# Mixer projections in blocks of 1024 columns, two of eight k-tile pairs with seven products, PE and ACT in a hand-written order, two sums moved to accumulating DMA

## The chip, the cores and the metric

One core of a Trainium2 chip runs the whole program. The metric is the device time of one execution in microseconds (us), the median of three runs. The core's engines work side by side and wait for each other through semaphores: TensorE (PE, matmuls and transposes), VectorE (DVE), ScalarE (ACT), GpSimd (POOL), and SyncE (SP), which here only issues the loads of weights. Operands lie in SBUF, results of PE in 8 banks of PSUM, each 128 partitions x 512 float32. All DMA queues share 16 DMA engines.

## The reference

One residual block on 256 tokens, model width 2048, float32:

```python
u = rms_norm(h, g_mix)
q, k, v, q_idx, k_idx, w_idx, z, xbc, dt_raw = split(u @ w_in)
y_attn = dsa_attention(rope(q), rope(k), v, rope(q_idx), rope(k_idx), w_idx)
# Mamba-2: conv and silu on xbc -> xs (4096 wide), B, C; 8 groups of 8 heads of 64, state 128
decay = exp(where(causal, acum[:, None] - acum[None, :], -inf))
y = (C B^T * decay) @ (xs * dt) + d_skip * xs
y = y * silu(z);  y_ssm = y * rsqrt(mean(y*y over the group) + eps) * g_norm
gates = sigmoid(u @ w_gate)
h = h + (gates[0] * (y_attn @ w_attn_branch) + gates[1] * (y_ssm @ w_ssm_branch)) @ w_out
h = h + (silu(gate) * up) @ w_ffn_out      # gate, up = split(rms_norm(h) @ w_ffn_in)
out = rms_norm(h, g_final)
```

The scan over chunks of 64 is computed in the kernel as one causal 256 x 256 product per head: three 128 x 128 tiles of decay a head, 128 x 384.

## The kernel before

**A projection.** 256 tokens are two row blocks (t) of 128; 2048 rows of a weight are 16 k-tiles of 128. The activation tile is the stationary operand, 512 columns of a weight are the moving one, and each product is made of three matmuls, hi x hi, hi x lo and lo x hi, so that float32 precision is kept. `gemm` makes 512 columns for both row blocks, in chunks of 4 k-tiles (1 MB): SP loads `raw`, ACT copies it to `hi` (L196, two 128x1024 copies a chunk), DVE subtracts `lo` (L197), PE does L165, L166 and L167 for each k-tile and row block (24 matmuls a chunk of 128x512). Four `mm` banks hold two gemms, so that one is read while the next is made; two banks (`tr`) take transposes, two (`sd`) small products. Four pairs of `hi`/`lo` tiles are in turn. In this text a *block* is 1024 columns of a projection, a *group* one of the 8 SSM groups, and `ssm_out` the product of a group's output with its 512 rows of w_ssm_branch (`w_sb`): 96 matmuls.

**The order of the work.** The program is written as a straight sequence, and Tile's scheduler orders each engine's instructions, with the weight loads and splits at high priority. The sequence: the small columns of w_in (`w_a`), then B and C (2048 columns of `w_m`), the index columns (`w_i`, two gemms of 384), eight groups (the x gemm of the group, `ssm_out` of the group before, the z gemm), k and v, four attention blocks (a q gemm of 512, a gate gemm of 512, the attention of 4 heads), `w_g` gates, `w_ab`, `w_o`, and the feed-forward block (FFN).

**The FFN's sevens.** In the FFN (`w_f`, L696 to L900) most chunks are made with seven products in place of eight for each 2 x 2 set of tiles (Strassen-Winograd): DVE forms differences of weight tiles (`ta` L749, `tb` L750, each then split like a weight, L730 and L731) and later adds the banks of the products together (L876). Its matmuls are L808 and its transposes L846. The change does not touch this code.

**A group's decay, `ssm_x`.** The running sums `acum` of a group's 8 heads lie in DRAM; POOL loads them to all partitions (`abc`), DVE forms 24 differences of 128x128, ACT takes the exponential, DVE multiplies by the masked scores `cbm`:

```python
nc.gpsimd.dma_start(abc..., acum_d[g * HPG : (g + 1) * HPG, :]...partition_broadcast(P))      # L481
nc.vector.tensor_scalar(E[:, hh, lo : lo + P], av[:, ao : ao + P], dcols[:, i, h : h + 1], 0.0, op, ALU.min)   # L504, 24 a group
nc.scalar.activation(E, E, AF.Exp)                                                             # L507, 128x1536, 2 a group
nc.vector.tensor_tensor(E, E, cbm.unsqueeze(1).broadcast_to([P, 4, 384]), ALU.mult)            # L508
```

**A group's output.** `y*y` is summed over 512 columns (L547 and a small matmul), POOL makes 1/sqrt of it (`rsg`, L133 to L144), and `ssm_out` scales its banks by it while it adds them to `acc`, which stays in SBUF over all groups:

```python
nc.scalar.activation(a, ps[t], AF.Copy, scale=r[:, t : t + 1])                  # L561, group 0
nc.vector.scalar_tensor_tensor(a, ps[t], r[:, t : t + 1], a, ALU.mult, ALU.add) # L563, groups 1 to 7
```

Of the kernel before, what the change touches and what calls it, by code (L numbers as in the profile page):

```python
# [41 lines left out]

C_GM = 0
# [21 lines left out]
def hybrid_block(ctx, tc, xt, x, consts, cols, heads, gfin, w_a, w_i, w_m, w_g, w_ab, w_sb, w_o, w_f1, w_f2, out):  # L65
# [12 lines left out]
    dp = ctx.enter_context(tc.tile_pool(name="dp", bufs=1, space=bass.MemoryType.DRAM))  # L78
    pctx = ctx.enter_context(ExitStack())
# [22 lines left out]
    def sd_t(shape, name="sd"):  # L102
        return sdp.tile(shape, F32, tag="sd", name=nm(name))
# [16 lines left out]
    tri = kc[:, K_TRI : K_TRI + P]  # L120
# [26 lines left out]
    xtra = []  # L147
    turn = [0]

    def hl_tiles():  # L150
        turn[0] += 1
        if xtra and turn[0] % 5 == 0:
            return xtra[0].tile([P, 1024], F32R, tag="hi", name=nm("hi")), xtra[0].tile([P, 1024], F32R, tag="lo", name=nm("lo"))
        return whi.tile([P, 1024], F32R, tag="hi", name=nm("hi")), wlo.tile([P, 1024], F32R, tag="lo", name=nm("lo"))

    def gemm(w, first, N, nk, lhs, before=None, late=0):


        ps = [mm.tile([P, 512], F32, tag="mm", name=nm("mm")) for _ in range(T)]
# [76 lines left out]
    u_hi = [big_t([P, 8, S], F32R, name="uh") for _ in range(2)]  # L236
    u_lo = [big_t([P, 8, S], F32R, name="ul") for _ in range(2)]

    def u_chunk(c, part=0):

        if c == 0:
            ks = (0, 2) if part == 0 else (2, 4)
        else:
            ks = (4 * c, 4 * c + 4)
        with tc.high_priority(PRE):
            load_xt(*ks)
            if c == 0 and part == 0:
# [28 lines left out]
    ps = gemm(w_a, 0, 400, KT, lhs_u, u_chunk)  # L276
# [17 lines left out]
    with tc.high_priority(PRE):  # L294
        sqp = sd_t([P, T])
        for t in range(T):
            for i in range(2):
                nc.tensor.matmul(sqp[:, t : t + 1], part[:, i, t * P : (t + 1) * P], onec, start=(i == 0), stop=(i == 1))
        ssq = sm.tile([P, T], F32, tag="ssq", name="ssq_x")
        nc.vector.tensor_copy(ssq, sqp)  # L300
        nc.vector.tensor_copy(rstd, rstd_of(ssq, D, "rs0"))
# [30 lines left out]
    wk0 = mid_t([P, 1024], name="wk0")  # L332
    wk1 = mid_t([P, 1024], name="wk1")
    kdup = wk0[:, 0:256].rearrange("p (t n) -> p t n", t=T)
    dtok = wk0[:, 256:384].rearrange("p (t n) -> p t n", t=T)
    dl, e1, rest = wk0[:SH, 384:640], wk0[:SH, 640:896], wk0[:SH, 896:1024]
    r1, r2, ones, ea = wk1[:SH, 0:256], wk1[:SH, 256:512], wk1[:SH, 512:640], wk1[:SH, 640:641]
    qi_a = mid_t([P, T, 256], name="qia")
    for t in range(T):
        nc.scalar.activation(dtok[:, t, :], ps[t][:, 336:400], AF.Copy, scale=rs(t))  # L340
        nc.scalar.activation(widx[:, t, :], ps[t][:, 320:336], AF.Copy, scale=rs(t))
        rope_apply(kdup[:, t, 0:64], ps[t][:, 256:320], t, 1, 32)
        nc.vector.tensor_copy(kdup[:, t, 64:128], kdup[:, t, 0:64])
# [3 lines left out]
    tp = tr_t([P, S])
    for t in range(T):
        nc.tensor.transpose(tp[:SH, t * P : (t + 1) * P], dtok[:, t, :], ident)
    nc.scalar.activation(dl, tp[:SH, :], AF.Identity, bias=headp[:, 0:1])  # L350
    nc.scalar.activation(e1, dl, AF.Abs)
    nc.scalar.activation(e1, e1, AF.Exp, scale=-1.0)
    nc.scalar.activation(ea, headp[:, 1:2], AF.Exp)
    nc.vector.tensor_scalar_add(r1, e1, 2.0)
    nc.vector.reciprocal(r1, r1)
    nc.vector.tensor_tensor(r1, r1, e1, ALU.mult)
    nc.vector.tensor_tensor(r2, r1, r1, ALU.mult)
# [10 lines left out]
    nc.vector.tensor_scalar(rest, dl[:, 0:P], -1.0, dl[:, P - 1 : P], ALU.mult, ALU.add)
    acum_d = dp.tile([SH, S], F32, name="acum_d")
    nc.gpsimd.dma_start(acum_d, dl)  # L370
    tp = tr_t([P, 5, SH])
    for i, src in enumerate((r1[:, 0:P], r1[:, P:S], dl[:, 0:P], dl[:, P:S], rest)):
        nc.tensor.transpose(tp[:, i, :], src, ident[:SH, :SH])
    dcols = cp.tile([P, 5, SH], F32, name="dcols")
    nc.vector.tensor_copy(dcols, tp)


    kbd = mid_t([P, 2, S], name="kbd")
    nc.gpsimd.memset(kbd, 0.0)
    tp = tr_t([P, S])  # L380
    for t in range(T):
        nc.tensor.transpose(tp[:, t * P : (t + 1) * P], kdup[:, t, :], ident)
    nc.vector.tensor_copy(kbd[0:64, 0, :], tp[0:64, :])
    nc.vector.tensor_copy(kbd[64:128, 1, :], tp[64:128, :])
    kbd_h = mid_t([P, 2, S], F32R, name="kbdh")
    kbd_l = mid_t([P, 2, S], F32R, name="kbdl")
    split(kbd_h, kbd_l, kbd)
# [28 lines left out]

    index_pairs(qi_a, 2, 12)


    def conv_block(ps, cb, dst):  # L420

        xk = ev_t([P, T, 512], "xk")
        for t in range(T):
            nc.scalar.activation(xk[:, t, :], ps[t], AF.Copy, scale=rs(t))
        for h in range(2):
            tp = tr_t([P, 2, S])
            for c in range(2):
                for t in range(T):
                    o = (2 * h + c) * P
                    nc.tensor.transpose(tp[:, c, t * P : (t + 1) * P], xk[:, t, o : o + P], ident)  # L430
            for c in range(2):
                ch = cb * 4 + 2 * h + c
                a = dst[:, 2 * h + c, :]
                nc.scalar.activation(a, tp[:, c, :], AF.Identity, scale=ccol(C_CW, 3 * 48 + ch), bias=ccol(C_CB, ch))
# [131 lines left out]
    for g in range(GROUPS):  # L566
# [3 lines left out]
        if pend is not None:  # L570
            ssm_out(*pend)
# [495 lines left out]
```

## Time and profile before

| | before |
|---|---|
| time, median of 3 runs | 1971.53 us (1970.67 to 1971.98) |
| span of the profiled execution | 1967.9 us |
| PE busy | 1954.5 us (99%) |
| DVE busy | 1499.9 us (76%) |
| ACT busy | 1066.8 us (54%) |
| POOL busy | 36.2 us (2%) |
| moved by DMA | 375.71 MB, mean 191 GB/s |

The span is 3.6 us under the median. In the span the stages lie so: `w_a`, B, C and index to about 185 us, eight groups to 748 (each takes 72.2 us), k and v to 820, attention to 1021, gates to 1108, `w_ab` to 1172, `w_o` to 1256, FFN to the end. In a group of rows, "x424 | 517.7, 1223 | 310.4" means 424 instructions, 517.7 us busy in all, 1223 ns for one by itself, and 310.4 us of idle time of that engine just ahead of them. One by itself can be longer than its part of the busy time, since an instruction begins before the one ahead has wholly ended. In a table by windows each row gives the busy time of PE, of the weight loads (PEld), DVE, ACT and POOL, then the granted clock of PE, the busy share of the DMA engines and what they moved in GB/s.

### The profile page before, as it was taken

To read this page: it belongs to the slowest core of one execution; us is meant where nothing else is said; L and a number is where in the kernel's file an instruction comes from. 1 tells how busy PE (TensorE), PEld (TensorE's weight loads), DVE (VectorE), ACT (ScalarE), POOL (GpSimd) and SP (SyncE) were. 2 spreads that over 40 slices of the span, in tenths; PEclk is the share of its full clock that TensorE was granted. 3 is DMA by queue.
4 is the path that set the end of the run, shared out by engine and by line. 5 is a ranking of instruction groups with operands and counts; after the bars stand their busy time and mean duration, and the time that the engine had idled before them with its cause. 6 is when DMAs were issued, how large, how long until landed. Compare 5 with 4: busy or idle time off the path is not lost. (4 is left out here: it accounts for less than half of the span.)

```text
span 1967.9 us, 23619 instructions
## 1 busy us (share of the span) xinstructions
PE 1954.5 (99%) x9095; PEld 1619.2 (82%) x9095; DVE 1499.9 (76%) x2050; ACT 1066.8 (54%) x1291; POOL 36.2 (2%) x87
## 2 busy tenths in 40 slices
PE   9999999999999999999999999999999999999998
PEld 7898888888888888888888888788888888888886
DVE  7898867778778766666654556788989999899964
ACT  6575564654654544555554445565555665555553
POOL 0000000000000000000000000000000000000000
PEclk9999999999999999999999999999999999999999
DMA  7645555555554545544555555455545555555553
GB/s 276 233 151 177 189 195 187 190 195 171 193 203 160 193 171 192 182 163 168 185 185 195 184 193 206 154 198 212 193 178 208 213 194 213 192 195 213 212 193 128
DMA packets 54432, 375.71 MB, mean 191 GB/s; under 512 B 6304, under 2 KB 6816, under 8 KB 10672
## 3 DMA queue, kind: packets, MB, share of 16 engines
q1 hardware_dynamic: 51120, 360.86, 51.8%
q0 software_dynamic: 1968, 11.60, 1.7%
q10 hardware_dynamic: 1232, 1.75, 0.2%
q8 instruction: 71, 1.16, 0.2%
q14 instruction: 41, 0.34, 0.1%
HBM read 372.02 MB, written 2.16 MB: 190 GB/s over the span
## 5 line engine op out<-in xcount | busy, mean ns | idle before, releaser
L197 DVE TENSOR_TENSOR lo<-raw,hi 128x1024 fp32r<-128x1024 f32 (+3 forms) x449 | 540.5, 1207 | 314.6 <-ACT hi L196 313.1
L196 ACT ACTIVATE hi<-raw 128x1024 fp32r<-128x1024 f32 (+3 forms) x449 | 468.8, 1047 | 529.9 <-PE mm L167 463.4
L166 PE MATMUL mm<-lo,uh 128*128 128x512 f32 (+2 forms) x1184 | 461.0, 389 | 0.0
L167 PE MATMUL mm<-hi,ul 128*128 128x512 f32 (+2 forms) x1184 | 458.2, 388 | 0.2 <-DVE ul L218 0.2
L165 PE MATMUL mm<-hi,uh 128*128 128x512 f32 (+2 forms) x1184 | 453.2, 389 | 1.0 <-ACT hi L196 1.0
L730 ACT ACTIVATE hi<-raw 128x1024 fp32r<-128x1024 f32 x240 | 232.8, 978 | 138.7 <-PE p L808 103.0
L808 PE MATMUL p<-hi,opa 128*128 128x512 f32 x924 | 306.4, 390 | 0.0
L731 DVE TENSOR_TENSOR lo<-raw,hi 128x1024 fp32r<-128x1024 f32 x240 | 265.0, 1119 | 19.9 <-ACT hi L730 19.1
L165 PEld LDWEIGHTS mm<-hi,uh 128*128 128x128 f32 x1184 | 222.5, 188 | 44.5 <-ACT hi L196 1.9
L167 PEld LDWEIGHTS mm<-hi,ul 128*128 128x128 f32 x1184 | 222.8, 188 | 42.5 <-DVE ul L218 0.5
L166 PEld LDWEIGHTS mm<-lo,uh 128*128 128x128 f32 x1184 | 222.9, 188 | 41.0 <-DVE lo L197 0.3
L808 PEld LDWEIGHTS p<-hi,opa 128*128 128x128 f32 x924 | 173.4, 188 | 35.6
L808 PE MATMUL p<-lo,opa 128*128 128x512 f32 x462 | 180.9, 392 | 0.7 <-DVE lo L731 0.7
L808 PE MATMUL p<-hi,act 128*128 128x512 f32 x416 | 132.5, 390 | 0.0
L808 PE MATMUL p<-hi,opb 128*128 128x512 f32 x352 | 127.2, 391 | 1.0 <-ACT opf L695 0.8
L808 PEld LDWEIGHTS p<-lo,opa 128*128 128x128 f32 x462 | 86.7, 188 | 19.7 <-DVE lo L731 1.9
L166 PE MATMUL mm<-lo,yh 128*128 128x512 f32 x256 | 100.4, 392 | 0.0
L167 PE MATMUL mm<-hi,yl 128*128 128x512 f32 x256 | 100.4, 392 | 0.0
L165 PE MATMUL mm<-hi,yh 128*128 128x512 f32 x256 | 100.1, 395 | 0.0
L808 PEld LDWEIGHTS p<-hi,act 128*128 128x128 f32 x416 | 78.1, 188 | 16.4 <-ACT hi L730 0.3
L730 ACT ACTIVATE hi<-tb 128x1024 fp32r<-128x1024 f32 x45 | 47.7, 1059 | 76.7 <-PE p L808 45.7
L808 PE MATMUL p<-lo,act 128*128 128x512 f32 x208 | 80.6, 391 | 0.0
(283 smaller groups left out, 2533.2 us busy)
## 6 DMA issues: line engine op xcount, KB each, us to landing
raw<-in_w_f_dram SPq DMA_DIRECT2D x132, 1024.0 KB, 4.8
raw<-in_w_m_dram SPq DMA_DIRECT2D x104, 1024.0 KB, 4.8
raw<-in_w_sb_dram SPq DMA_DIRECT2D x32, 1024.0 KB, 4.8
raw<-in_w_g_dram SPq DMA_DIRECT2D x32, 1024.0 KB, 4.8
raw<-in_w_ab_dram SPq DMA_DIRECT2D x16, 1024.0 KB, 4.8
raw<-in_w_o_dram SPq DMA_DIRECT2D x16, 1024.0 KB, 4.8
abc<-acum_d POOLq DMA_DIRECT2D x8, 1024.0 KB, 5.2
raw<-in_w_i_dram SPq DMA_DIRECT2D x8, 768.0 KB, 4.3
```

The costliest lines, as they stand in the source:

```text
L165: nc.tensor.matmul(o, lh, rh, start=(kt == 0), stop=False)
L166: nc.tensor.matmul(o, lh, rl, start=False, stop=False)
L167: nc.tensor.matmul(o, ll, rh, start=False, stop=(kt == nk - 1))
L196: hi_ops.append(nc.scalar.activation(hi[:, o], src[:, o], AF.Copy))
L197: nc.vector.tensor_tensor(lo[:, o], src[:, o], hi[:, o].bitcast(F32), ALU.subtract)
L730: nc.scalar.activation(hi, src, AF.Copy)
L731: nc.vector.tensor_tensor(lo, src, hi.bitcast(F32), ALU.subtract)
L808: nc.tensor.matmul(ps[i], x, y, start=start and j == 0, stop=left[i] == 0)
```

## The change

All projections of u (`w_m`, `w_i`, `w_g`) are made in blocks of 1024 (`w_i`: 768) columns; q and the gate columns of an attention block share one block, as do x and z of a group. A block is made as a 2 x 2 set of results: two row blocks by two column halves, in all four `mm` banks. Its 16 k-tiles are four quads of 4, each two chunks of 1 MB; ORDER sets the order of the eight chunks, and MIX marks quads 0 and 1, whose first chunk (one pair of k-tiles) is made with 7 products of three matmuls instead of 8 (`sevens`). Four of the seven products go to banks of their own (1, 5, 6, 7), which are the four `trp` banks; `sdp` is gone, and transposes and small products share `trp`. DVE adds the banks together at the end of the block (`add`). The first two blocks (B and C) are plain; 15 blocks of 1024 and the one of 768 have sevens.

`ssm_out` is made as two plain blocks of 1024 columns. ACT copies its scaled banks to `sums`, and POOL adds these by an accumulating DMA to `acc_d` in DRAM, which is read back after the last group. The decay starts from a mask that a DMA loads into `E`; a second, accumulating DMA adds the rows of `acum`, and ACT takes the exponential with the per-partition part as a bias, 16 instructions a group. The masked score product is one ACT copy. The sum of squares of x comes from loads of x and ACT's accumulator, not from transposed squares and small matmuls; that of y from two adds.

PE and ACT run in the order in which the program is written (`manual_schedule`); the steps of a group are generators that are resumed after counted matmuls (`tick`). DVE, POOL and SP are ordered by the scheduler as before. FFN, `w_ab` and `w_o` keep their code, without the extra `hi`/`lo` pair that came in every fifth time.

```diff
+MIX = (1, 1, 0, 0)
+ORDER = ((2, 0), (2, 1), (0, 0), (1, 0), (0, 1), (1, 1), (3, 0), (3, 1))
+NHL = 5
...
-    whi = ctx.enter_context(tc.tile_pool(name="whi", bufs=4))
-    wlo = ctx.enter_context(tc.tile_pool(name="wlo", bufs=4))
+    whi = ctx.enter_context(tc.tile_pool(name="whi", bufs=NHL))
+    wlo = ctx.enter_context(tc.tile_pool(name="wlo", bufs=NHL))
-    ev = ctx.enter_context(tc.tile_pool(name="ev", bufs=2))
+    ev = ctx.enter_context(tc.tile_pool(name="ev", bufs=4))
...
-    trp = pctx.enter_context(tc.tile_pool(name="trp", bufs=2, space=bass.MemoryType.PSUM))
-    sdp = pctx.enter_context(tc.tile_pool(name="sdp", bufs=2, space=bass.MemoryType.PSUM))
+    trp = pctx.enter_context(tc.tile_pool(name="trp", bufs=4, space=bass.MemoryType.PSUM))
...
+    manual.enter_context(tc.manual_schedule(engines={mybir.EngineType.PE, mybir.EngineType.Activation}))
...
+            if seven:
+                yield from ask()
+                flush()
+                ta, tb = (mid_t([P, 1024], name="ts")[:, : 2 * N] for _ in range(2))
+                nc.vector.tensor_tensor(ta, tile_of(2, 2), tile_of(1, 2), ALU.subtract)
+                part(tile_of(0, 2), 0, 1)
...
+                part(ta, 4, 5)
+                nc.vector.tensor_tensor(tb[:, :N], tile_of(3), ta[:, :N], ALU.subtract)
+                nc.vector.tensor_tensor(tb[:, N:], tile_of(0), tb[:, :N], ALU.subtract)
...
+                part(tb, 6, 7)
...
+                part(tile_of(3), 3)
...
+        for x, part in ((a[0], 0), (a[0], 1), (a[1], 0)):
+            for c, b in uses:
+                left[c] -= 1
+                nc.tensor.matmul(ps[c], x, b[part], start=c in begun, stop=left[c] == 0)
...
+            for m, (c, l, r) in enumerate(((1, 0, 1), ((0, 0), 2, 0), (7, 1, 5), (5, 8, 4), (6, 9, 6), ((1, 0), 3, 7), ((0, 1), 12, 3))):
+                products(ps, left, get, op_u(q, l), [(c, operand(n, r))])
...
+                    if c == 1:
...
+                        nc.scalar.activation(x[1], ps[1], AF.Copy)
+                    elif c == 6:
+                        add(2, 6, 1)
+                        add(3, 7, 2)
+                        add(4, 5, 3)
+                        add(2, 5, 2)
...
+        xin = [big_t([P, D], name="xin") for _ in range(T)]
+        for t in range(T):
+            nc.scalar.dma_start(xin[t], x[t * P : (t + 1) * P, :])
...
+                nc.scalar.activation(v, v, AF.Square, accum_out=sq2[:, t, h : h + 1])
...
+                for i, e in ((2, Es[q][:, hh, 0:S]), (3, Es[q][:, hh, S:384])):
+                    nc.scalar.activation(e, e, AF.Exp, bias=dcols[:, i, h : h + 1])
...
+                    nc.vector.tensor_tensor(e, e, cbm.unsqueeze(1).broadcast_to([P, 2, 384]), ALU.mult)
...
+                nc.gpsimd.dma_start(E, mask.unsqueeze(1).broadcast_to([P, 4, 384]))
...
+            nc.gpsimd.dma_start(
+                E.rearrange("p h s -> p (h s)"),
+                acum_d[h : h + 4, :].rearrange("h s -> (h s)").partition_broadcast(P),
+                accum_op=ALU.add,
+            )
...
-        nc.vector.tensor_reduce(part, y.rearrange("p k s -> p s k"), AX.X, ALU.add)
+        nc.vector.tensor_tensor(part, xs[:, 0, :], xs[:, 1, :], ALU.add)
...
+                    nc.scalar.activation(part[:, t, n * 512 : (n + 1) * 512], p, AF.Copy, scale=res[2][:, t : t + 1])
...
-                    nc.vector.scalar_tensor_tensor(a, ps[t], r[:, t : t + 1], a, ALU.mult, ALU.add)
+                    nc.gpsimd.dma_start(d, part[:, t, :], accum_op=ALU.add)
```

On PE, before: the middle of a group's gemm. `mm_4366` and `mm_4367` are the banks of row blocks 0 and 1, `hi`/`lo` the halves of the weight, `uh`/`ul` those of u.

```order
L165 MATMUL mm_4366<-hi_4438,uh_104 128x512
L166 MATMUL mm_4366<-lo_4439,uh_104 128x512
L167 MATMUL mm_4366<-hi_4438,ul_106 128x512
L165 MATMUL mm_4367<-hi_4438,uh_104 128x512
L166 MATMUL mm_4367<-lo_4439,uh_104 128x512
L167 MATMUL mm_4367<-hi_4438,ul_106 128x512
```

On PE, now: the middle of the first sevens chunk of a block. `ua` are tiles of u, `us` sums of them, `p1`, `p7` and `p5` the banks of products 1, 7 and 5, `mm_465` a bank of the result. `ua` holds both halves of u, so that the first and third matmul of a product read alike.

```order
L489 MATMUL p1_484_2708<-hi_462_2597,ua_4_103 128x512
L489 MATMUL p1_484_2708<-lo_463_2598,ua_4_103 128x512
L489 MATMUL p1_484_2708<-hi_462_2597,ua_4_103 128x512
L489 MATMUL mm_465_2610<-hi_462_2597,ua_4_103 128x512
L489 MATMUL mm_465_2610<-lo_463_2598,ua_4_103 128x512
L489 MATMUL mm_465_2610<-hi_462_2597,ua_4_103 128x512
L489 MATMUL p7_487_2721<-hi_471_2641,ua_4_103 128x512
L489 MATMUL p7_487_2721<-lo_472_2642,ua_4_103 128x512
L489 MATMUL p7_487_2721<-hi_471_2641,ua_4_103 128x512
L489 MATMUL p5_488_2725<-hi_471_2641,us_322 128x512
L489 MATMUL p5_488_2725<-lo_472_2642,us_322 128x512
L489 MATMUL p5_488_2725<-hi_471_2641,us_322 128x512
```

Each product has three matmuls as before; a chunk of such a kind has 21 in place of 24, from four `hi`/`lo` tiles in place of two, and its products fill banks that transposes used.

On ACT, before: around the exponential of a group. `E` are the decay tiles, `z` the gate of the group.

```order
L196 ACTIVATE hi_3142<-raw_3140 128x1024
L196 ACTIVATE hi_3158<-raw_3140 128x1024
L507 ACT_TABLE_LOAD
L507 ACTIVATE E_3407<-E_3407 128x1536
L196 ACTIVATE hi_3220<-raw_3218 128x1024
L507 ACTIVATE E_3433<-E_3433 128x1536
L196 ACTIVATE hi_3236<-raw_3218 128x1024
```

On ACT, now: in `ssm_out`, where the exponentials of one group and the bank copies of the group before stand.

```order
L427 ACTIVATE hi_4973<-raw_4854 128x1024
L796 ACTIVATE E_4910<-E_4910,dcols 128x256
L796 ACTIVATE E_4910<-E_4910,dcols 128x128
L743 ACTIVATE xsc_4939<-tr_5001,colp 128x256 x2
L900 ACTIVATE sums_4916<-mm_4917,rsg_4986 128x512
L900 ACTIVATE sums_4916<-mm_4918,rsg_4986 128x512
L427 ACTIVATE hi_5029<-raw_4854 128x1024
L427 ACTIVATE hi_5040<-raw_4902 128x1024
L900 ACTIVATE sums_4916<-mm_4947,rsg_4986 128x512
L900 ACTIVATE sums_4916<-mm_4948,rsg_4986 128x512
```

Two long exponentials a group have become sixteen short ones, and the copies of banks (`sums`), which wait for PE and for POOL's `rsg`, now stand among the splits of weights (`hi`).

On POOL, before: one group's part.

```order
L481 DMA abc_3929<-acum_d 128x2048
L133 TENSOR_SCALAR rv_3207<-ssq_3205 128x2
L135 TENSOR_TENSOR rsg_3209<-rv_3207,neg_half 128x2
L137 TENSOR_TENSOR rq_3211<-rsg_3209 128x2
L142 TENSOR_TENSOR rq_3211<-rq_3211,rv_3207 128x2
```

On POOL, now: one group's part. `L905` adds to the sums in DRAM, `L810` and `L812` fill `E` for the next group.

```order
L905 DMA acc_d<-sums_4309 128x1024 x2
L810 DMA E_4910<-in_mask_dram 128x4x384
L810 DMA E_4913<-in_mask_dram 128x4x384
L905 DMA acc_d<-sums_4444 128x1024
L812 DMA E_4910<-acum_d 128x1536
L905 DMA acc_d<-sums_4444 128x1024
L812 DMA E_4913<-acum_d 128x1536
L142 TENSOR_SCALAR rv_4984<-ssq_4982 128x2
L144 TENSOR_TENSOR rsg_4986<-rv_4984,neg_half 128x2
```

Eight DMA issues stand where one stood, ahead of the next `rsg`.

More of the change, by code (lines that the diff above doesn't have):

```diff
@@ L293, in hybrid_block @@
     rstd = cp.tile([P, T], F32, name="rstd")
[L294 to L301, printed above, removed]
     def rs(t):
@@ L347, in hybrid_block @@
[L347 to L357, printed above, removed]
@@ L368, in hybrid_block @@
[L368 to L379, printed above, removed]
@@ L380, in hybrid_block @@
[L380 to L384, printed above, removed]
+    dcols = cp.tile([P, 4, SH], F32, name="dcols")
+    acum_d = dp.tile([SH, 384], F32, name="acum_d")
     kbd_h = mid_t([P, 2, S], F32R, name="kbdh")
     kbd_l = mid_t([P, 2, S], F32R, name="kbdl")
-    split(kbd_h, kbd_l, kbd)
     isc = [cp.tile([P, P * (t + 1)], F32, name=f"isc{t}") for t in range(T)]
@@ new lines, in hybrid_block, with pump, operand, give @@
+    feeder = feed()
+    def pump():
+        next(feeder, None)
+    at = [0]
+    def operand(n, key):
+        if key not in ready.get(n, ()):
+            pump()
+        flush()
+        return ready[n][key]
+    def give():
+        room[0] += 1
+        pump()
+    def products(ps, left, alloc, a, uses):
+        begun = set()
+        for c, b in uses:
+            if c not in ps:
+                ps[c] = alloc(c)
+                begun.add(c)
+        for x, part in ((a[0], 0), (a[0], 1), (a[1], 0)):
+            for c, b in uses:
+                left[c] -= 1
+                nc.tensor.matmul(ps[c], x, b[part], start=c in begun, stop=left[c] == 0)
+                begun.discard(c)
@@ new lines, in plain_chunk @@
+    def plain_chunk(ps, left, alloc, a_of, n, cuts, edge, done=None, close=False):
+        steps = [(k, t) for k in range(2) for t in range(T)]
+        if edge:
+            steps.sort(key=lambda u: u[1])
+        for k, t in steps:
+            hi, lo = operand(n, k)
+            products(ps, left, alloc, a_of(k, t), [((t, i), (hi[:, o : o + m], lo[:, o : o + m])) for i, (o, m) in enumerate(cuts)])
+            if t == T - 1:
+                give()
+            if done is not None and k == 1:
+                done(t)
+            closing[0] = close and (k, t) >= (0, 1)
+            tick(6)
+        closing[0] = False
@@ new lines, in bank, with plain @@
+    def bank(n):
+        return lambda c: mm.tile([P, 512], F32, tag="mm", name=nm("mm"))[:, :n]
+    def plain(nk, N, lhs, done):
+        ps = {}
+        left = {(t, i): 3 * nk for t in range(T) for i in range(2)}
+        for c in range(nk // 2):
+            n = at[0]
+            at[0] += 1
+            first, last = c == 0, c == nk // 2 - 1
+            plain_chunk(ps, left, bank(N), lambda k, t: lhs(2 * c + k, t), n, ((0, N), (N, N)), first or last,
+                        (lambda t: done(t, ps[t, 0], ps[t, 1])) if last else None)
@@ L425, in conv_block, with scaled, conv_steps @@
+    for _ in range(3):
+        pump()
+    head = job_of(head_steps())
+    def scaled(v):
+        for t in range(T):
+            ins = nc.scalar.activation(v[t], v[t], AF.Copy, scale=rs(t))
+        return ins
+    def conv_steps(xk, cb, dst, behind=None, gap=12):
         for h in range(2):
```

689 lines of the change are left out of this document (489 added, 200 removed).

## Prediction

> **What bounds the kernel now.** I read the busy times first, then the waits of PE, then the windows of each stage, and last the grouped rows, which give prices.
>
> ```profile
> span 1967.9 us, 23619 instructions
> PE 1954.5 (99%) x9095; PEld 1619.2 (82%) x9095; DVE 1499.9 (76%) x2050; ACT 1066.8 (54%) x1291; POOL 36.2 (2%) x87
> ```
>
> PE is idle for 13.4 us of 1967.9. Its longest waits by line:
>
> ```profile
> PE warm L273 <- DVE wz L270: 1.2, 1, 1.2
> PE mm L165 <- ACT hi L196: 1.0, 1, 1.0
> ```
>
> So no other engine holds PE up: a matmul taken away is time taken away, as long as the others still keep ahead. How far ahead they are differs by stage. The rows give PE, PEld, DVE, ACT and POOL busy, PE's clock, DMA share, GB/s; the windows are the head, the index search, one SSM group, the four attention blocks, and a stretch of the FFN.
>
> ```profile
> 0.00:35.00 35.00, 32.63 (x146) 27.44 (x147) 25.31 (x33) 25.08 (x36) 0.32 (x6) 1.00 0.86 324
> 107.00:147.00 40.00, 40.00 (x219) 37.42 (x218) 37.00 (x99) 28.80 (x36) 0.00 (x0) 1.00 0.49 163
> 307.30:379.50 72.20, 72.20 (x353) 59.38 (x352) 55.19 (x86) 38.85 (x44) 2.62 (x6) 1.00 0.54 189
> 820.00:1021.00 201.00, 201.00 (x939) 167.54 (x939) 131.54 (x163) 114.97 (x175) 2.23 (x4) 1.00 0.51 175
> 1350.00:1700.00 350.00, 350.00 (x1570) 288.90 (x1569) 320.44 (x379) 201.38 (x227) 0.00 (x0) 1.00 0.57 202
> ```
>
> PE is full in the last four at full clock. The reader should keep two of them: DVE is busy for 320.44 of 350 us (92%) in the FFN, and 37.00 of 40 (93%) in the index search, and PE loses nothing. A busy DVE alone does not delay PE; only work that comes late does.
>
> **PE: what goes.** The price of a 512-column matmul is read from the chain, where 546 of them follow each other:
>
> ```profile
> 1441.77 124.15 PE p L808 x546
> ```
>
> 124.15/546 = 0.2274 us. Each sevens chunk leaves out three. Fifteen blocks with two such chunks give 90 matmuls, 90 x 0.2274 = 20.5 us. The 768-column block gives 6 of 384 columns at 0.2274 x 384/512 = 0.171, 1.0 us. The sum of squares of x by matmuls goes:
>
> ```profile
> L298 PE MATMUL sd<-onec,part 128*128 128x1 f32 x8 | 1.0, 228 | 0.0
> ```
>
> With it and one transpose fewer, 1.1 us. Together 22.6 us; the FFN's count stays. All of it lies on the path, because PE has no idle time to hide it. Against it stands whatever PE now waits for.
>
> **DVE.** Rows for the prices:
>
> ```profile
> L197 DVE TENSOR_TENSOR lo<-raw,hi 128x1024 fp32r<-128x1024 f32 x424 | 517.7, 1223 | 310.4 <-ACT hi L196 308.9
> L749 DVE TENSOR_TENSOR ta<-raw 128x1024 f32<-128x1024 f32 x45 | 55.0, 1223 | 25.9 <-DMA raw<-in_w_f_dram 25.4
> L750 DVE TENSOR_TENSOR tb<-raw,ta 128x512 f32<-128x512 f32 x45 | 30.8, 685 | 0.0
> L876 DVE TENSOR_TENSOR xa<-p,xa 128x512 f32<-128x512 f32 x44 | 30.1, 685 | 0.8 <-PE p L808 0.5
> L504 DVE TENSOR_SCALAR E<-abc,dcols 128x128 f32<-128x128 f32 x192 | 39.5, 280 | 0.0
> L563 DVE SCALAR_TENSOR_TENSOR acc<-mm,rsg,acc 128x512 f32<-128x512 f32 x56 | 39.3, 742 | 0.4 <-PE mm L167 0.4
> L547 DVE TENSOR_REDUCE ysq<-xsc 128x256 f32<-128x1024 f32 x8 | 16.3, 2034 | 0.0
> ```
>
> A block's two sevens chunks need 3.5 `lo` each in place of 2 (a half tile at 0.685): +1.9 a chunk, 3.8. `ta` and two `tb`: 1.223 + 1.370 = 2.6 a chunk, 5.2. Eight bank additions, 8 x 0.685 = 5.5. A block thus costs DVE 14.5 us more. A group loses 39.5/8 = 4.9 (L504), 39.3/7 = 5.6 (L563), some 1.5 of mask products and of the sum of y*y (two adds of 512 and 256 columns, about 0.7 and 0.4 by L876, for the 2.0 of L547, and two masks of 128 columns, 0.28 each by L504), and pays 0.4 for the decay product in four pieces. Net 55.2 + 14.5 + 0.4 - 12.0 = 58.1 of a shorter 69.5 us, 84%: below what the FFN bears. An attention block has no such relief: 131.54/4 = 32.9, + 14.5 = 47.4, of 201/4 - 6 x 0.2274 = 48.9, 97%. That is above what any row shows free of waits. Inside a sevens chunk DVE's 6.9 us (4.3 `lo`, 2.6 differences) stand against PE's 21 x 0.2274 = 4.8; two in a row put DVE 4.2 us behind, which the five tile pairs must cover. The FFN does the same with chunks of this kind. I take 2 to 3 us for the four attention blocks (bounds 0, as in the FFN; and 14, if the excess over the FFN's 92% is wholly lost: 47.4/0.92 - 48.9 = 2.6 a block, 11, and 3 for the index search), nearest to the FFN row.
>
> **ACT.** Prices:
>
> ```profile
> L196 ACT ACTIVATE hi<-raw 128x1024 fp32r<-128x1024 f32 x424 | 448.8, 1060 | 517.6 <-PE mm L167 453.1 <-issue 40.4 <-ACT yh L217 5.1
> L507 ACT ACTIVATE E<-E 128x1536 f32<-128x1536 f32 x16 | 23.7, 1481 | 0.1
> L629 ACT ACTIVATE sc<-sc,mx 128x256 f32<-128x256 f32 x16 | 8.0, 498 | 0.0
> L629 ACT ACTIVATE sc<-sc,mx 128x128 f32<-128x128 f32 x16 | 6.2, 387 | 0.9 <-DVE mx L626 0.9
> L561 ACT ACTIVATE acc<-mm,rsg 128x512 f32<-128x512 f32 x8 | 5.4, 680 | 3.5 <-PE mm L167 3.5
> L434 ACT ACTIVATE xsc<-tr,colp 128x256 f32<-128x256 f32 x32 | 17.6, 553 | 13.1 <-PE tr L430 13.0
> ```
>
> The sixteen exponentials (L629 is the same function with a per-partition bias in 256 and 128 columns) cost 8 x 0.885 = 7.1 against 2 x 1.481 = 3.0; the eight copies to `sums` 8 x 0.680 = 5.4; the splits of sevens +3.4; copies of a bank and of `cbm` +0.9. A group: 38.85 + 13.8 = 52.6 of 69.5, 76%. On average harmless, but in `ssm_out` it bunches: 96 matmuls (21.8 us) and 8 transposes and small ones (1.9, the transposes at 0.44 for four by the chain row below) are 23.7 us of PE, in which ACT has 8 splits (8 x 1.06), 7.1 of exponentials, 5.4 of copies, a table load of 1.28, four scalings of convolution tiles (4 x 0.55) and 0.5 for `cbm`, 24.9 us. And here lateness counts: a block uses all four `mm` banks, so the next block's first row block waits until ACT has emptied two of them, covered by 12 matmuls = 2.7 us less 2 x 0.68 of copying, 1.4 us to spare for whatever stands ahead on ACT. POOL's `rsg` must be there as well:
>
> ```profile
> 449.32 0.19 POOL L133 TENSOR_SCALAR rv<-ssq 128x2 f32<-128x2 f32 x1 [27.09 <-DVE ssq L552]
> ...
> 451.73 0.19 POOL L144 TENSOR_TENSOR rsg<-rsg,rq 128x2 f32<-128x2 f32 x1
> ```
>
> ```profile
> 1565.92 0.44 PE tr L846 x4
> ```
>
> From 449.32 to 451.92 `rsg` takes 2.6 us. Bounds for a group: 0, and 24.9 - 23.7 = 1.2 for ACT. I take 0.4, nearer to zero, since exponentials wait for nothing and can be left behind; 8 x 0.4 = 3 us.
>
> ```profile
> 346.70 1.28 ACT L507 ACT_TABLE_LOAD   x1
> 347.99 1.49 ACT L507 ACTIVATE E<-E 128x1536 f32<-128x1536 f32 x1
> ```
>
> The table load takes 1.28 us, and the exponential starts 0.01 us behind it; I count 1.28. The Trainium skill ("ScalarE: Activation LUTs", What ACT_TABLE_LOAD costs) adds a drain of about 1.38 us to each switch; these rows show no gap of that size behind the load. By that rule ACT would have about 26.3 us in `ssm_out`, and the sum would come out some 11 us later.
>
> **DMA.** Rows of issues (KB each, median us to landing):
>
> ```profile
> raw<-in_w_m_dram SPq DMA_DIRECT2D x104, 1024.0 KB, 4.8
> abc<-acum_d POOLq DMA_DIRECT2D x8, 1024.0 KB, 5.2
> ```
>
> A group moved 189 GB/s x 72.2 us = 13.65 MB at a share of 0.54, so a full DMA moves some 350. Now `abc` (1.05 MB) goes; two masks, two accumulations into `E` (each 0.79 MB) and four into DRAM (each 0.52) come: 13.65 - 1.05 + 5.24 = 17.84 MB in 69.5 us, of which 3.67 accumulate. No row shows an accumulating DMA. If its bytes cost as a copy's (f = 1) the share is 0.73; at f = 2, 0.88. The DMA is full at f = 2.8. The `E` DMAs are issued a group ahead and weights two chunks (10.9 us) ahead against 4.8 to land, so below that I cost it at nothing; the cover is gone from f = 2.8 on, and the next lateness is then the weights. The lower end, a gain, has no row that speaks for it. I take f between 1 and 2, nearest to the copies. On POOL, `rsg` is queued behind an accumulation into `E` that waits for its mask; both stand where `ssm_out` ends, a block of 186 matmuls (42 us) ahead of the next `rsg`, against 5.2 to land.
>
> The Trainium skill ("DMA: Bandwidth & Descriptors", Rules for kernel authors) has an accumulating DMA read its destination too. No run here shows it; by that alone f would be 2, and the sum stays.
>
> **Head.** Loads of x add 2.1 MB to a stretch that already runs at a share of 0.86 and 324 GB/s; at 324/0.86 = 377 GB/s they take 5.6 us, and 35 x 0.14 = 4.9 are free. I take 2 to 3 us for this and the first, uncovered sevens (bounds 0 and 5.6).
>
> **Sum.** 1967.9 - 22.6 + 8 (3 in `ssm_out`, 2.5 each in attention and head) = 1953.3 us of span. The median stood 3.6 above the span: 1957.
>
> **The rivals.**
> - *No added waits.* PE's hand order hides all: 1967.9 - 22.6 + 3.6 = 1949. For it, the FFN row; against it, 97% of DVE in attention.
> - *DVE binds.* Attention and index lose 14 us by the bound above: 1949 + 14 + 3 for `ssm_out` = 1966, perhaps 1963 to 1970. Decided by whether DVE falls behind at the end of an attention block, with banks waiting to be added.
> - *ACT late at bank releases.* Each group loses the 1.2, and up to 1.4 more where a table load or an exponential stands ahead of a bank copy: 8 x 2.5 = 20, 1949 + 20 = 1969. If a change of tables holds ACT for longer than the load's 1.28, this is where it shows: 1.4 more a switch is 8 x 1.4 = 11 us, 1968. The 0.01 us ahead of L507 speaks against it, so it gets 0.02 of ACT's chance. (That is what the Trainium skill's drain, in "ScalarE: Activation LUTs", would do here.)
> - *Slower: the accumulating DMAs fill the DMA.* At f = 3.5 a group needs 17.84 + 2.5 x 3.67 = 27.0 MB, 77 us at 350 GB/s, against 69.5: 8 x 7.6 = 61 and 1953 + 61 = 2014. Break-even with before at 72.2 us a group is f = 3.0. For it: additions are work that a copy does not have, and nothing here prices them. Against it: 3.67 of 17.84 MB only, and the issues are early.
>
> **How the numbers follow.** Within 0.2% (4 us) a measurement of this kernel cannot tell a change. The forecast, small waits (1949 to 1963), 0.55; no added waits 0.12; DVE binds 0.13; ACT late 0.07; DMA full 0.13. Faster: the first two, 0.67, and part of DVE's and ACT's, 0.08, together 0.75; same 0.11; slower: DMA full and 0.01 of the rest, 0.14. The range must leave out no more than 2 in 10: from 1947, just under the case without waits, to 1974, the end of ACT late; what lies above is DMA full.
>
> **What the profile after would show.** PE's matmul count down by some 100, and its idle time near 20 us in place of 13. A group of 69 to 70 us, an attention block of 49 to 50. ACT's `hi` and DVE's `lo` among PE's waits for 1 to 3 us a stage, bank copies (L900) for under 1 a group. The DMA share in a group 0.73 to 0.9. The FFN stretch as before. I am wrong if weight loads land much later than 4.8 us in the groups (DMA), if PE waits for `rsg` or L900 by more than 2 us a group, if PE waits for additions of banks in attention, or if the hand order makes PE stand behind one late transpose while matmuls that are ready stand after it, which no row of the old order can show.

## The result: 1996.15 us, slower by 1.2%, and the profile after

| | before | after |
|---|---|---|
| median of 4 runs | 1971.59 us | 1996.15 us |
| ratio, 95% interval | | 1.0124 (1.0109 to 1.0138) |
| span of the profiled execution | 1967.9 us | 1995.8 us |
| one SSM group (from one `ssm_out` to the next) | 72.2 us | 75 to 78 us, one 83.4, the last 72.4 |
| start of the FFN | 1256.7 us | 1286.4 us |

The first lines of the page of the changed kernel:

```profile
span 1995.8 us, 23976 instructions
PE 1952.8 (98%) x8990; PEld 1600.0 (80%) x8990; DVE 1604.6 (80%) x2109; ACT 1177.9 (59%) x1564; POOL 93.2 (5%) x149
```

PE has 105 records fewer, as the change says, but 43.0 us of the span idle in place of 13.4. Its busy time fell by only 1.7 us, though 22.6 us of matmuls are gone, so the idle time is not all that was lost: a matmul's record lasts 394 ns on the mean (L489) while the next begins 227 ns behind it, so that shorter delays, and matmuls at a lower clock, count as busy. Its waits:

```profile
PE yp L848 <- DVE xdt L836: 16.1, 7, 4.4
PE mm L489 <- ACT sums L900: 2.7, 2, 2.1
PE mm L168 <- ACT hi L199: 2.2, 3, 0.9
PE sqp L886 <- DVE ysq L882: 2.1, 1, 2.1
```

The largest is for a product of the SSM groups, `yp`, that waits for `xdt` (x times dt), which DVE makes. It is not in the sum of the prediction. The same group as a window, before and after, and a stretch of the FFN after:

```profile
451.70:524.00 72.30, 72.30 (x354) 59.44 (x354) 55.20 (x86) 38.95 (x44) 2.85 (x8) 1.00 0.55 190
```

```profile
494.00:570.50 76.50, 74.04 (x347) 58.85 (x346) 56.64 (x74) 49.45 (x71) 9.99 (x14) 0.98 0.75 234
...
1380.00:1700.00 320.00, 320.00 (x1435) 264.82 (x1434) 292.56 (x348) 186.19 (x211) 0.00 (x0) 1.00 0.57 203
```

The FFN is as before. In the group DVE is busy for only 56.64 of 76.50 us, and the DMA share of 0.75 looks harmless. Cut into stretches of 10 us, most of the same group looks otherwise:

```profile
504.00:514.00 10.00, 9.88 (x42) 7.40 (x41) 7.29 (x11) 8.50 (x14) 3.44 (x6) 1.00 0.69 165
514.00:524.00 10.00, 10.00 (x46) 8.27 (x45) 6.97 (x8) 7.67 (x13) 2.22 (x3) 1.00 0.95 311
524.00:534.00 10.00, 10.00 (x46) 8.27 (x45) 8.94 (x10) 8.99 (x13) 2.12 (x3) 1.00 1.02 263
534.00:544.00 10.00, 10.00 (x50) 8.26 (x49) 7.18 (x9) 3.91 (x5) 0.00 (x0) 1.00 1.04 304
544.00:554.00 10.00, 7.66 (x36) 5.26 (x35) 7.12 (x9) 4.01 (x4) 0.00 (x0) 0.83 0.94 354
554.00:564.00 10.00, 10.00 (x56) 7.77 (x55) 5.35 (x9) 3.55 (x5) 0.00 (x0) 1.00 0.36 115
```

For 40 us, from 514 to 554, the DMA engines are full; then they are two thirds idle. In the last of these stretches PE stands for 2.34 us, and its granted clock falls to 0.83. The queue of POOL shows what begins the burst:

```profile
506.61 0.92 POOL L905 DMA_DIRECT2D acc_d<-sums  x1 [1.59 <-ACT sums L900]
509.84 0.87 POOL L905 DMA_DIRECT2D acc_d<-sums  x1 [2.31 <-ACT sums L900]
510.40 1.11 POOL L810 DMA_DIRECT2D E<-in_mask_dram  x1
520.51 0.78 POOL L810 DMA_DIRECT2D E<-in_mask_dram  x1 [9.00 <-DMA acc_d<-sums]
521.27 0.96 POOL L905 DMA_DIRECT2D acc_d<-sums  x1
523.50 0.88 POOL L812 DMA_DIRECT2D E<-acum_d  x1 [1.27 <-DMA E<-in_mask_dram]
524.07 1.19 POOL L905 DMA_DIRECT2D acc_d<-sums  x1
530.91 0.85 POOL L812 DMA_DIRECT2D E<-acum_d  x1 [5.65 <-DMA E<-in_mask_dram]
```

All eight DMAs of a group are issued within 25 us. The weights of the mixed block meanwhile land in 10.1 us (window 514 to 546, median) in place of 4.8:

```profile
raw<-in_w_m_dram SPq DMA_DIRECT2D x4, 1024.0 KB, 10.1
```

Then one wait hangs on the other: ACT waits for a weight, DVE's `lo` waits for ACT, and `xdt` stands behind that `lo` on DVE. ACT, then DVE, then PE:

```profile
546.05 2.00 ACT L427 ACTIVATE hi<-raw 128x1024 fp32r<-128x1024 f32 x2 [4.21 <-DMA raw<-in_w_m_dram]
```

```profile
547.14 2.36 DVE L429 TENSOR_TENSOR lo<-raw,hi 128x1024 fp32r<-128x1024 f32 x2 [1.46 <-ACT hi L427]
549.42 0.68 DVE L836 TENSOR_TENSOR xdt<-tr,dcols 128x512 f32<-128x512 f32 x1
```

```profile
542.51 0.60 PE L835 MATMUL tr<-kc,xsc 128*128 128x128 f32 x4
...
550.16 1.97 PE L848 MATMUL yp<-E,xdt 128*64 128x128 f32 x12 [2.34 <-DVE xdt L836]
552.07 1.22 PE L489 MATMUL mm<-hi,ua 128*128 128x512 f32 x2
...
555.16 0.63 PE L489 MATMUL mm<-hi,ua 128*128 128x512 f32 x2
```

The transposes (`tr`) that this `xdt` reads ended at 543.11 us, 6.3 us before DVE began it; in between DVE was idle for 1.46 us and then made the two late `lo`. So the lateness reaches PE through the order of DVE, which the scheduler sets. No run puts `xdt` ahead of `lo`: what that alone would give back is open. After its pause of 2.34 us PE takes 1.22 us for two matmuls, and 0.63 three us later.

### The profile page after: what moved, and what is told of

Its sections match the earlier page's. It is cut to its first block, busy times and chain, and to the rows that moved or that the text cites. A ratio compares the mean times of both kernels' runs of the same rounds, so it can differ in the third digit from the quotient of the medians.

```text
span 1995.8 us, 23976 instructions
## 1 busy us (share of the span) xinstructions
PE 1952.8 (98%) x8990; PEld 1600.0 (80%) x8990; DVE 1604.6 (80%) x2109; ACT 1177.9 (59%) x1564; POOL 93.2 (5%) x149
## 3 DMA queue, kind: packets, MB, share of 16 engines
q0 software_dynamic: 11152, 47.29, 10.2%
## 4 chain that ended last, share of the span: by engine, by line
PE 79%; DVE 9%; DMA 6%; ACT 4%; issue 2%; POOL 0%; SPq 0%; DVEq 0%; ACTq 0%; POOLq 0%
PE p L1199 31%; PE mm L489 29%; DMA raw<-in_w_m_dram 5%; PE mm L169 4%; PE mm L170 4%; PE mm L168 4%; DVE lo L429 4%; PE p L489 2%; ACT hi L427 1%; PE yp L848 1%; PE lg L979 1%; PE tr L1237 0%; DVE xsc L750 0%; DVE E L800 0%; DVE xb L530 0%
## 5 line engine op out<-in xcount | busy, mean ns | idle before, releaser
L489 PE MATMUL mm<-hi,ua 128*128 128x512 f32 (+1 forms) x1920 | 563.4, 394 | 2.6 <-DVE xb L530 1.5
L427 ACT ACTIVATE hi<-raw 128x1024 fp32r<-128x1024 f32 (+1 forms) x352 | 349.4, 1008 | 266.0 <-PE mm L489 161.0
L429 DVE TENSOR_TENSOR lo<-raw,hi 128x1024 fp32r<-128x1024 f32 (+1 forms) x352 | 403.5, 1161 | 120.4 <-ACT hi L427 119.7
L489 PEld LDWEIGHTS mm<-hi,ua 128*128 128x128 f32 x1920 | 354.0, 189 | 72.9 <-issue 3.0
L489 PE MATMUL mm<-lo,ua 128*128 128x512 f32 (+1 forms) x960 | 301.0, 389 | 0.0
L489 PEld LDWEIGHTS mm<-lo,ua 128*128 128x128 f32 x960 | 181.1, 189 | 37.3 <-DVE lo L429 0.3
L200 DVE TENSOR_TENSOR lo<-raw,hi 128x1024 fp32r<-128x1024 f32 (+2 forms) x97 | 115.1, 1194 | 85.3 <-ACT hi L199 85.2
L199 ACT ACTIVATE hi<-raw 128x1024 fp32r<-128x1024 f32 (+2 forms) x97 | 99.6, 1035 | 110.2 <-PE mm L170 98.4
L427 ACT ACTIVATE hi<-ts 128x1024 fp32r<-128x1024 f32 (+1 forms) x64 | 65.7, 1042 | 45.8 <-DVE ts L451 24.9
L489 PE MATMUL mm<-hi,yh 128*128 128x512 f32 x256 | 86.4, 410 | 3.6 <-ACT sums L900 2.7
L489 PE MATMUL mm<-lo,yh 128*128 128x512 f32 x256 | 79.5, 391 | 0.0
```

Of the source, the lines that this page charges most:

```text
L199: hi_ops.append(nc.scalar.activation(hi[:, o], src[:, o], AF.Copy))
L200: nc.vector.tensor_tensor(lo[:, o], src[:, o], hi[:, o].bitcast(F32), ALU.subtract)
L427: nc.scalar.activation(hi, src, AF.Copy)
L429: lows.append(lambda: nc.vector.tensor_tensor(lo, src, hi.bitcast(F32), ALU.subtract))
L489: nc.tensor.matmul(ps[c], x, b[part], start=c in begun, stop=left[c] == 0)
```

## The experiments

Theory 1: the added DMA work comes in a burst that makes the weights late. Theory 2: the sevens fill DVE, or hold the shared banks, and the DMA has no part. Medians of each kernel follow; the kernel before had 1971.1 to 1971.9 beside them.

**Without the adding.** Both accumulating DMAs overwrite.

```diff
-                accum_op=ALU.add,
...
-                    nc.gpsimd.dma_start(d, part[:, t, :], accum_op=ALU.add)
+                    nc.gpsimd.dma_start(d, part[:, t, :])
```

> Left out: the adding. The DMAs of acum rows into E and of the sums into DRAM have the same places, bytes and queue, but overwrite; the exponents' biases are a constant. Theory 1 (in the 40 us after each ssm_out the DMA engines are full, because an accumulated byte costs about two, so the weights of the mixed block land late): a burst that needs some 46 us of DMA time in 40 comes down to some 37, weights land in 5 to 6 us in place of 10, most waits in the groups go: 1958 to 1972. Theory 2 (DVE is too full in the mixed block, from the sevens and the order on it, and the second xdt comes late whatever the DMA does): 1988 to 1997, and PE still waits some 16 us for xdt.

1973.41 us (1.0011, 1.0002 to 1.0020), 22.7 less. PE waits for `xdt` once, 1.5 us. The group takes 72.4:

```profile
478.90:551.30 72.40, 72.32 (x348) 57.99 (x347) 56.67 (x74) 49.87 (x71) 7.91 (x14) 1.00 0.67 247
```

The time is 1.4 us above theory 1's range. Theory 1 holds for these 22.7 us, and DVE's work, 56.67, is what it was. But the time stays some 24 us above what fewer matmuls should give (1949): theory 1 isn't all.

**Without POOL's DMAs.** E is set by POOL, the sums go nowhere.

```diff
-                nc.gpsimd.dma_start(E, mask.unsqueeze(1).broadcast_to([P, 4, 384]))
...
+            nc.gpsimd.memset(E, -1.0e4)
...
-                    nc.gpsimd.dma_start(d, part[:, t, :], accum_op=ALU.add)
```

> Left out: all DMAs of POOL in the groups but the first group's sums (E is set by two POOL instructions, sums of groups 1 to 7 go nowhere). Theory 1: a group takes 70.8 to 71.5 us (72.2 less six matmuls of 0.2274), the whole 1946 to 1954. Theory 2: waits for xdt stay, 1980 to 1997.

1973.28 us: between the two ranges, some 20 above theory 1's. Beside the kernel without the adding (1973.41) the bytes that are only copied cost nothing here; it is the adding that does.

**Without the sums' DMAs alone.**

```diff
-                    nc.gpsimd.dma_start(d, part[:, t, :], accum_op=ALU.add)
```

> Left out: the accumulating DMAs of the sums alone, for groups 1 to 7. They are 2.1 of 5.2 MB and stand ahead of E's masks, which wait for their buffers. Theory 1: the burst needs some 35 us of 40 and may begin earlier: 1955 to 1972. Theory 2: 1988 to 1997.

1977.81 us (1.0031, 1.0019 to 1.0044), 18.3 less, above the expected range: most of the burst's cost goes with 4 of its 6 additions.

**One seven.**

```diff
-MIX = (1, 1, 0, 0)
+MIX = (1, 0, 0, 0)
```

> One chunk with seven products a block in place of two: PE 48 matmuls more (10.7 us), DVE 4.5 us less a block, the DMAs the same. Theory 1: the burst stays, a block gets 0.7 us longer in which the same bytes must land, so between 1994 (all hidden in the waits) and 2005. Theory 2: the waits for xdt shrink with DVE's load, 1975 to 1992.

1969.45 us (0.9990, 0.9981 to 0.9999): 26.7 us less with 10.7 us more of matmuls, below the ranges of both theories. All additions are there, with a DMA share of 0.80, and PE has no wait left in this group:

```profile
475.80:547.80 72.00, 72.00 (x350) 58.62 (x349) 52.00 (x69) 47.95 (x70) 9.52 (x14) 1.00 0.80 248
```

So the burst alone does not delay PE; it does beside a second seven.

**Sevens apart.**

```diff
-ORDER = ((2, 0), (2, 1), (0, 0), (1, 0), (0, 1), (1, 1), (3, 0), (3, 1))
+ORDER = ((2, 0), (2, 1), (0, 0), (0, 1), (1, 0), (1, 1), (3, 0), (3, 1))
```

> The two chunks with seven products of a block no longer stand one behind the other: the plain chunk of quad 0 stands between them (the four shared banks stay taken 24 matmuls longer). Theory 1 (two sevens in a row leave DVE some 4 us behind and the five hi/lo pairs empty, and only then does a weight that lands 5 us late reach PE): waits for xdt mostly go, 1972 to 1986. Rival (the late weights cost the same wherever the sevens stand): 1992 to 1999.

2012.72 us, worse by 16.6: missed. DVE gets a pause between the sevens, but the four shared banks are taken for 24 matmuls longer. PE's waits are now spread over several steps of a group, as they would be if what needs these banks comes late; the run with the banks held longer, below, tests that with one seven:

```profile
PE mm L489 <- ACT sums L900: 9.4, 15, 1.6
PE mm L489 <- DVE yl L873: 8.8, 8, 1.3
PE yp L848 <- DVE xdt L836: 6.1, 6, 1.8
PE mm L489 <- DVE lo L429: 6.0, 5, 2.9
```

**One seven without the adding.** Both edits together.

> One chunk of seven a block, and the DMAs of E and the sums overwrite in place of adding (left out: the adding, and the biases are a constant). Theory 1: the DMA's lateness is covered with one seven already, so the time stays within 3 us of the 1969.5 of one seven with the adding. Rival (the two costs stand by themselves, 23 us for the adding whatever the sevens): 1945 to 1950.

1968.15 us, 1.3 under one seven with the adding, within the noise; with two sevens, leaving out the adding gained 22.7. The two costs are not independent: late weights reach PE beside the second seven and hardly beside one alone. That this seven uses up the lead (the work that DVE, ACT and the banks have ready ahead of PE) is the reading that fits.

**No accumulating DMA, whole.** Sums in SBUF by DVE as before the change, E by one plain DMA, the mask added by POOL.

```diff
+                        nc.vector.scalar_tensor_tensor(a, p, r, a, ALU.mult, ALU.add)
...
+                nc.gpsimd.tensor_tensor(E[:, :, lo : lo + P], E[:, :, lo : lo + P], tri.unsqueeze(1).broadcast_to([P, 4, P]), ALU.add)
```

> The whole computation, two sevens in a row, without any accumulating DMA: the sums over groups are kept in SBUF by DVE as before the change, E is loaded by one plain DMA and POOL adds the mask to its two triangular parts. DVE has 5.6 us more a group, ACT 5.4 less, DMA some 7 MB-equivalents less. Theory 1: as the kernel without POOL's DMAs (1973), less what ACT's lateness at the banks cost, if that counts: 1962 to 1976. Theory 2 (DVE's load binds): 1976 to 1990.

1986.41 us: theory 2's range. DVE now empties the banks of `ssm_out`, and PE waits for it:

```profile
PE mm L493 <- DVE acc L905: 5.3, 14, 2.7
```

**No sevens,** and **no sevens and no adding.** Plain blocks in the plain order of chunks, copied out by ACT; the sums of tiles of u (`us`) that only sevens need are not made.

```diff
-MIX = (1, 1, 0, 0)
-ORDER = ((2, 0), (2, 1), (0, 0), (1, 0), (0, 1), (1, 1), (3, 0), (3, 1))
+MIX = (0, 0, 0, 0)
+ORDER = tuple((q, part) for q in range(4) for part in range(2))
...
+        plain(KT, N, lhs_u, done)
```

> No sevens at all: every block is plain, its banks are copied out by ACT; hand order, shared banks, 1024-column blocks and accumulating DMAs stay. PE has 21.5 us of matmuls more than the changed kernel, about as many as before the change. If the order by hand, the four banks a block and the accumulating DMAs cost nothing by themselves: 1968 to 1973. If the 25 us that are lost without the adding belong to the order and the banks: 1985 to 1998. If they belong to the sevens: 1968 to 1976.

> No sevens (1976.1), and the DMAs of E and the sums overwrite in place of adding (left out: the adding, and the biases are a constant). If the adding is hidden without sevens, as it is with one (1.3 us), 1973 to 1977: then the 5 us over the kernel before belong to the order by hand, the four banks a block and the moved sums. If the adding costs here what the kernel lost: 1968 to 1972.

1976.11 us (1.0024, 1.0013 to 1.0035) and 1975.81 us (1.0023, 1.0013 to 1.0032). Here too the adding is hidden; order by hand, blocks of 1024, shared banks and the moved work together cost some 4 us over the kernel before.

**Two sevens, no adding, no differences of weight tiles.** The splits read the loaded tiles; left out is what that makes of the products.

```diff
-                part(ta, 4, 5)
+                part(tile_of(2, 2), 4, 5)
...
-                part(tb, 6, 7)
+                part(tile_of(1, 2), 6, 7)
```

> As the kernel whose POOL DMAs overwrite in place of adding (1973.4), and the differences of weight tiles are left out too: the second and third split of a sevens chunk read the loaded tiles themselves. PE has the same matmuls in the same order, DVE 5.2 us less a block, and no split waits for a difference. Of the 17 us that the second seven loses there: if DVE's work and the chain through the differences are the cause, 1955 to 1963; if the four shared banks are (steps of a group are held while they are taken, and come bunched behind), 1970 to 1975.

1967.27 us, 6.1 under the 1973.41 with the differences: between the two ranges. DVE's work, or the chain through the differences, is a part, not the whole. In the groups nothing changes, 72.3 us; the gain lies outside them.

**One seven, banks held longer.**

```diff
-            sevens[0] = made < N7
+            sevens[0] = True
...
+                sevens[0] = False
```

> One seven a block (1969.5), but the steps of the groups that need a shared bank are held through the next, plain chunk as well, about as long as two sevens hold them. DVE's work is that of one seven. If the holding of the banks is what the second seven costs: 1976 to 1988. If it is DVE's work: 1967 to 1972.

1981.95 us, 12.5 over the kernel with one seven, with the same instructions. The group goes from 72.0 to 73.3 us with DVE as little loaded as there:

```profile
482.40:555.70 73.30, 73.14 (x350) 58.43 (x349) 52.56 (x69) 48.04 (x69) 10.01 (x14) 1.00 0.78 244
```

The holding of the shared banks has a cost of its own (the adding is in this kernel too, so the 12.5 may hold a part of it).

**E later.** The changed kernel, whole; E's DMAs are issued behind a small copy on POOL that waits for ACT's copy of the second seven's first bank.

```diff
                         nc.scalar.activation(x[1], ps[1], AF.Copy)
+                        mid_block[0] = paced(x[1])
...
-            with tc.issue_after(paced(xk[0]) if q else first_e) if g == 0 else nullcontext():
+            with tc.issue_after((paced(xk[0]) if q else first_e) if g == 0 else mid_block[0]):
```

> The changed kernel, whole; only the loads and additions of E are issued later, when the second seven of the next block has begun (some 25 us after now), so that they no longer follow the additions of the sums at once. The same bytes. If the burst is the cause of the 23 us that the adding costs: weights land in 5 to 8 us and the time is 1974 to 1986. If the adding costs the same wherever it stands: 1992 to 1999. If E then comes too late for the exponentials, ACT waits for it and the time is above 2000.

1974.36 us (1.0020, 1.0011 to 1.0030): 21.8 us less with the same bytes and the same additions; counted from the first sum's DMA, the four of E are issued 15 to 25 us later. The group takes 72.4 us at a mean share of 0.79, above the 0.75 of the changed kernel:

```profile
480.80:553.20 72.40, 72.29 (x348) 57.96 (x347) 56.62 (x74) 49.91 (x71) 10.22 (x15) 1.00 0.79 247
...
510.00:520.00 10.00, 10.00 (x45) 8.26 (x44) 8.55 (x10) 8.95 (x12) 0.00 (x0) 1.00 0.76 218
520.00:530.00 10.00, 10.00 (x49) 8.29 (x48) 10.00 (x12) 7.01 (x8) 1.83 (x3) 1.00 0.75 288
530.00:540.00 10.00, 10.00 (x63) 7.30 (x62) 6.04 (x9) 3.18 (x3) 1.80 (x2) 1.00 1.02 339
```

The share has a gap in the middle, and the weights of `w_m` land in 5.0 us (median of all) in place of 5.4. Those of `w_sb`, for `ssm_out`, land in 9.6 in place of 5.0, later than before:

```profile
raw<-in_w_m_dram SPq DMA_DIRECT2D x120, 1024.0 KB, 5.0
raw<-in_w_sb_dram SPq DMA_DIRECT2D x32, 1024.0 KB, 9.6
```

So the DMAs still make weights late, but now mostly those of `ssm_out`'s plain blocks, and `xdt` is no longer among PE's longest waits. This shows that the time at which the bytes move, and not their amount, is the cause of the 22 us.

**One seven and E later.**

> The whole computation with what the runs so far favour: one seven a block, and E loaded and added to in the middle of the next block. By the kernel with one seven whose DMAs overwrite (1968.2) the adding can give back no more than 1.3 us: 1966.5 to 1970. If the pacing brings E too late for the exponentials with one seven: above 1972.

1972.27 us (1.0005, 0.9996 to 1.0014): missed, 2.8 us above one seven alone, hardly clear of the noise. With one seven the adding cost only 1.3 us, so that there was little to give back; the first two groups got longer (78.0 and 74.6 us against 76.5 and 73.2, from one `ssm_out` to the next), and why is not settled. The best whole kernel remains the one with one seven, 0.1% under the kernel before, which is less than the 0.2% that the prediction set as the least that can be told.

## Why the prediction was wrong

The matmuls went as forecast: 105 records fewer are the 96 of the sevens (21.5 us) and nine small ones (1.1), the 22.6 us of the prediction. The term of 8 us for added waits failed; by the price of the matmuls, 47.1 us were lost. The runs split this, by steps from kernel to kernel (medians, whose intervals reach 2 to 3 us to either side, so that the 3.0 is hardly clear of them; matmuls by the prediction's price):

| step | matmuls | time | lost |
|---|---|---|---|
| before to no sevens, no adding | -1.1 | +4.2 | 5.3 |
| first seven (no adding) | -10.7 | -7.7 | 3.0 |
| second seven (no adding) | -10.7 | +5.3 | 16.0 |
| the adding, with two sevens | 0 | +22.7 | 22.7 |
| sum | -22.5 | +24.6 | 47.1 |

- *The accumulating DMAs.* The rival on the slower side named the resource and the sign to watch, weights that land late, but its point of decision was wrong. It set a group's bytes against a group's time and put the limit at 2.8 times a copy's cost. The price itself can now be worked out:

```profile
q0 software_dynamic: 11152, 47.29, 10.2%
```

```profile
q0 software_dynamic: 11152, 47.29, 6.4%
```

  (POOL's queue: packets, MB, share; after, and without the adding.) 6.4% of 1971.7 us are 126 us for 47.29 MB, 375 GB/s; 10.2% of 1995.8 are 204. The adding concerns 28 sums of 0.52 MB and 16 tiles of 0.79, 27.3 MB, 73 us at that rate and 150 with it: f = 2.1, where the prediction took f between 1 and 2, nearest to 1. At f = 2 it had 0.88 for the group and cost it at nothing. Right was the mean (0.74 to 0.78 measured in groups of 75 to 78 us), wrong the step from the mean to no cost: in the 40 us that matter the weights of a block (42 us long, 8.4 MB, 22 us of DMA at that rate) and the burst (5.2 MB, of which 3.7 are added and count twice, 24 us) need some 46, by estimate. The prediction's own 350 GB/s and f = 2 give 49 us for the same bytes in a block of 42 us, so the excess could be read beforehand. "The `E` DMAs are issued a group ahead" was read as cover; it put them right behind the sums, and issuing them later took back 21.8 us. The Trainium skill ("DMA: Bandwidth & Descriptors", Rules for kernel authors) has the adding read its destination too; the measured 2.1 fits that.
- *The second seven.* The prediction costed it by DVE's busy share and took the FFN as proof that two in a row do no harm. In attention DVE did not bind: 91% (136.61 of 149.80 us) in place of the 97% worked out.

```profile
888.30:1038.10 149.80, 148.78 (x694) 122.69 (x693) 136.61 (x182) 91.57 (x143) 2.16 (x4) 1.00 0.50 179
```

  Three attention blocks take 49.93 us each, one us above the 48.9 forecast. What a mixed block has and an FFN chunk hasn't are transposes and small products of a group that need the four banks of the sevens. While these are taken, the steps of the group are held and come late. The prediction's last sentence named the hand order as something "no row of the old order can show", and gave it no price; in the runs the held banks cost up to 12.5 us (one seven, held longer, with the adding), the differences 6.1. How the two make up the second seven's 16.0 us was not separated.
- *`ssm_out`.* Its 3 us match by luck: PE's visible waits for L900 are 2.7 us in all, but they are two waits in one group, not 0.4 in each.
- *The head,* 2.5 us: about right. PE idles for 4.1 of the first 35 us in place of 2.4, and for 1.2 more up to 200. The group in which the index search ends is the longest of all (83.4 us, a wait for `xdt` of 4.4 and two for L900), and no term stood for that.
- *A slip:* the group was said to shrink to 69.5 us. Six matmuls of 0.2274 make 70.8 of the 72.2; with it DVE's 84% becomes 82%.
- *The table load.* It begins 0.02 us behind the split ahead of it and is followed by the exponential within 0.01 us, so the drain that the Trainium skill ("ScalarE: Activation LUTs", What ACT_TABLE_LOAD costs) adds is not seen here:

```profile
498.16 1.06 ACT L427 ACTIVATE hi<-raw 128x1024 fp32r<-128x1024 f32 x1 [0.37 <-PE mm L489]
499.24 1.28 ACT L796 ACT_TABLE_LOAD   x1
500.53 0.80 ACT L796 ACTIVATE E<-E,dcols 128x256 f32<-128x256 f32 x2
```

Not settled: which part of the hand order and the shared banks costs the 5.3 us without sevens; how the second seven's 16.0 divides between the held banks and the differences, since the run that held the banks had the adding as well; and what an order of DVE with `xdt` ahead of the late `lo` would save.

## What to carry to other kernels

Set the work of a shared resource against the stretch in which it is issued, not against the loop's mean: a DMA share of 0.75 over 76 us was 1.0 over 40 and 0.36 after, and issuing four of eight DMAs 15 to 25 us later gave 22 us back. A saving in matmuls that is paid with lead (raw tiles held longer, shared banks taken, more splits) is worth its matmuls only as long as lead is left, so try it in halves: without the adding the first seven kept 7.7 of its 10.7 us, the second lost 5.3. When transfers are issued early, ask what they collide with, and what stands behind the late work on each engine.

## What the runs showed of the hardware

After three of PE's pauses for `xdt` the granted clock was about half for some us: 0.50 from 393.1 to 399.9 us, behind the pause of 4.4 us; 0.50 from 471.6 to 478.4, behind one of 2.8; and 0.51 from 550.1 to 553.5, behind the 2.34 us above. In windows of 10 us this reads as 0.83 there and as 0.66 at the longest:

```profile
390.00:400.00 10.00, 5.57 (x23) 4.07 (x22) 6.01 (x7) 4.00 (x4) 0.00 (x0) 0.66 0.80 288
```

In the next two groups pauses of 2.4 and 2.6 us were followed by no drop, so the length of the pause alone does not decide it:

```profile
570.50:645.70 75.20, 72.74 (x349) 58.06 (x348) 56.82 (x74) 49.74 (x71) 9.99 (x14) 1.00 0.78 238
645.70:720.90 75.20, 72.47 (x348) 57.85 (x347) 56.66 (x74) 49.48 (x71) 10.00 (x14) 1.00 0.77 238
```

Over the whole execution the mean clock was 0.994 against 0.998 before and 0.999 with one seven. By that (an estimate from these means) up to 0.004 x 1996 = 8 us of the loss are not waits but their echo.
